# Memory-head softmax weights of a hybrid decoder trunk: transposed by DMA as two planes of 16-bit halves instead of on TensorE

## The chip, the cores and the metric

The kernel runs as one program on one core of a Trainium2 chip. The metric is the time of one execution in microseconds (us) of device time; a smaller time is better. The engines are named as in the profile: PE is TensorE (PEld its weight loads), DVE is VectorE, ACT is ScalarE, POOL is GpSimd, SP is SyncE, which issues nearly all DMAs of this kernel. Lines such as L1320 are lines of the kernel before.

## What is computed

Two decoder layers on 512 tokens of width 1024, all in fp32: a half-step SwiGLU, a mixing block of three attention branches (8 stick-breaking heads, 8 forgetting heads, 4 memory heads), another half-step SwiGLU. The change is in the memory heads. Cut to what matters of the reference:

```python
def _memory_attention(q, k, v):        # 4 heads of width 128, 512 queries, 256 memory rows
    z = jnp.einsum('bhqd,bhkd->bhqk', q, k).astype(jnp.float32) * (q.shape[-1] ** -0.5)
    p = jax.nn.softmax(z, axis=-1)
    return jnp.einsum('bhqk,bhkd->bhqd', p.astype(v.dtype), v)
...
for l in range(DEPTH):                 # DEPTH = 2
    ...
    k_mem, v_mem = jnp.split(mem_n @ w_mem_kv[l], 2, axis=-1)
    o_mem = _memory_attention(_split_heads(q_mem, N_MEM_HEADS), _split_heads(k_mem, N_MEM_HEADS),
                              _split_heads(v_mem, N_MEM_HEADS))
```

So there are 2 layers x 4 heads = 8 memory heads in the program.

## The kernel before

**Precision.** A product of two fp32 matrices is made of three matmuls of rounded parts (`mm3`, L212 to L214): high x high, high x low, low x high. Whatever enters a product is first taken apart by `split`: ACT casts the value to its high part (L182), DVE subtracts that from the value for the low part (L183). With a scale the two lines are L185 and L186.

**The mixing block.** Long products (queries, keys, values, gates) are jobs of a queue `Q`; each job loads its weights (`raw_`), takes them apart (`wh_`, `wl_`, four buffers each) and runs its matmuls. Attention heads are generators that are woven between the jobs: a head yields `("wait", us)` where it expects other engines to need that long, and the weaver then puts so many us of matmuls of the jobs into PE's program before it goes on with the head. The waits are numbers in the code, not measured at run time. Most of the order of ACT, DVE and SP comes out of the scheduler that lays out the program; at run time each engine takes its instructions strictly in that order.

**A memory head** (`mem_head`). Its 512 x 256 scores lie in two PSUM banks (`zm`), each of two blocks of 128 queries x 256 memory rows. DVE finds the maxima (L1300, L1301), ACT makes the exponentials with their sums (L1304), DVE divides (L1306, L1309): the weights `pm`, two tiles of 128 x 512. Then comes a wait W_MM0. The second product needs the weights with memory rows on partitions, so TensorE transposes them: eight 128 x 128 blocks against an identity (L1320) into two PSUM banks, which `split` takes apart into the tile `ptm`. After a wait W_MM1 six matmuls (`pvm`) multiply `ptm` with the values `mv`, and `split` writes the head's output `om`.

**The order of the heads** (`mems`). The scores of head i+1 go before the rest of head i. In the last head, at its last wait, the program turns to the first stick-breaking head: jobs are run until that head's q and k are there, ACT's function table is changed to the sigmoid's (`functions`, an ACT_TABLE_LOAD at L196), and its scores (`zs`, L1210) are started.

**The stick-breaking heads** use a DMA for their transposes already. `turn_out` (L1152) has ACT copy the 16-bit halves of the words into two planes, `turn_over` (L1161) has SP issue a DMA that transposes both planes, and ACT joins the halves into words again (L1237):

```python
    def turn_out(words, w, planes):
        both = words[:, :w].bitcast(U16).rearrange("p (k h) -> p h k", h=2)
        nc.scalar.copy(planes[:, :w].bitcast(U16).rearrange("p (h k) -> p h k", h=2), both)
    def turn_over(planes, w, over):
        nc.sync.dma_start_transpose(over[:, :w].bitcast(U16).rearrange("p (r q) -> p r q", q=P), planes[:, :w].bitcast(U16))
```

Of the kernel before, what the change touches and what calls it, by code (L numbers as in the profile page):

```python
# [12 lines left out]
U16 = mybir.dt.uint16  # L13
# [5 lines left out]
P = 128  # L19
# [4 lines left out]
def kernel(  # L24
# [38 lines left out]
    nc = tc.nc  # L63
    _, S, D = x.shape
    M = mem.shape[1]
    L = w_in.shape[0]
    NT = S // P
    ND = D // P
    MT = M // P
# [4 lines left out]
    NMH = 4  # L74
# [24 lines left out]
    def tmp(name):  # L99
        return sb.tile([P, S], F32, tag="f32t", bufs=8, name=name)  # L100
# [3 lines left out]
    def stile(shape, tag, name, dt=F32R):  # L104
        return sb.tile(shape, dt, tag=tag, bufs=BUFS[tag], name=name)
# [4 lines left out]
    def pbank(tag, name):  # L110
        return ps.tile([P, S], F32, tag=tag, bufs=4, name=name)
# [67 lines left out]
    def split(h_ap, l_ap, src, scale=None, later=False):  # L179

        if scale is None:
            both = [nc.scalar.copy(h_ap, src)]  # L182
            make = lambda: nc.vector.tensor_tensor(l_ap, src, h_ap.bitcast(F32), ALU.subtract)  # L183
        else:
            both = [nc.scalar.activation(h_ap, src, AF.Copy, scale=scale)]  # L185
            make = lambda: nc.vector.scalar_tensor_tensor(l_ap, src, scale, h_ap.bitcast(F32), ALU.mult, ALU.subtract)  # L186
        if later:
            return make
        both.append(make())
        if Q.pinned:  # L190
            for ins in both:
                tc.keep_in_program_order(ins)
        return both
# [16 lines left out]
    def mm3(pt, lh, ll, rh, rl, start, stop, free=False):  # L210

        nc.tensor.matmul(pt, lh, rh, start=start, stop=False, skip_group_check=free)  # L212
        nc.tensor.matmul(pt, lh, rl, start=False, stop=False, skip_group_check=free)  # L213
        nc.tensor.matmul(pt, ll, rh, start=False, stop=stop, skip_group_check=free)  # L214
# [934 lines left out]
# [4 lines that stand above are left out]
# [6 lines left out]
    def turn_over(planes, w, over):  # L1159

        nc.sync.dma_start_transpose(over[:, :w].bitcast(U16).rearrange("p (r q) -> p r q", q=P), planes[:, :w].bitcast(U16))  # L1161
# [125 lines left out]
    def mem_head(q, ks, vs, hd, ot, name, begun):  # L1287
        scale = P ** -0.5
        pts = []
        for i2 in range(NT // 2):  # L1290
            pz = pbank("z", f"z{name}_{i2}")
            for e in range(2):
                i = 2 * i2 + e
                qs = slice(i * P, (i + 1) * P)
                kk = ks[hd // 2]
                mm3(pz[:, e * M:(e + 1) * M], q[:, 0, qs], q[:, 1, qs],
                    kk[:, 0, hd % 2], kk[:, 1, hd % 2], e == 0, e == 1)
            st = sb.tile([P, 4], F32, tag="st4", bufs=4, name=f"st{name}_{i2}")
            p = tmp(f"p{name}_{i2}")
            nc.vector.tensor_reduce(st[:, 0:2], pz[:].rearrange("p (e m) -> p e m", e=2), AX.X, ALU.max, negate=True)  # L1300
            nc.vector.tensor_scalar(st[:, 0:2], st[:, 0:2], scale, None, ALU.mult)  # L1301
            for e in range(2):
                c = slice(e * M, (e + 1) * M)
                nc.scalar.activation(p[:, c], pz[:, c], AF.Exp, bias=st[:, e:e + 1], scale=scale,  # L1304
                                     accum_out=st[:, 2 + e:3 + e])
            nc.vector.reciprocal(st[:, 2:4], st[:, 2:4])  # L1306
            for e in range(2):
                c = slice(e * M, (e + 1) * M)
                nc.vector.tensor_scalar(p[:, c], p[:, c], st[:, 2 + e:3 + e], None, ALU.mult)  # L1309
            pts.append(p)  # L1310
        yield ("pe", 1.3)
        yield ("wait", W_MM0)
        begun()
        tri = stile([P, 2, MT * S], "tri", "pt" + name)
        for kt in range(MT):
            pt = pbank("z", f"pt{name}_{kt}")
            for i in range(NT):
                a = (i % 2) * M + kt * P
                tc.keep_in_program_order(
                    nc.tensor.transpose(pt[:, i * P:(i + 1) * P], pts[i // 2][:, a:a + P], ident[:]))  # L1320
            c = slice(kt * S, (kt + 1) * S)
            split(tri[:, 0, c], tri[:, 1, c], pt[:])
        yield ("pe", 0.9)
        yield ("wait", W_MM1)
        pv = pbank("mm", "pv" + name)
        for kt in range(MT):
            c = slice(kt * S, (kt + 1) * S)
            vc = slice((hd % 2) * P, (hd % 2 + 1) * P)
            v = vs[hd // 2]
            mm3(pv[:], v[:, 0, kt, vc], v[:, 1, kt, vc], tri[:, 0, c], tri[:, 1, c], kt == 0, kt == MT - 1)  # L1330
        split(ot[:, 0], ot[:, 1], pv[:])
        yield ("pe", 1.3)

    W_SB0, W_SB1, W_SB2 = 7.0, 7.0, 5.0
    W_FX0, W_FX1 = 6.5, 4.7
    W_MM0, W_MM1 = 6.0, 6.0
    W_K = 4.0

    FOX = (2, 3, 0, 1)
# [28 lines left out]
    def mixing(l, src, ks, vs, rest, dst):  # L1368
# [177 lines left out]
        def run():  # L1546
            Q.until(marks["first"])
            for i in range(NT):
                nc.sync.dma_start(hsave[i], hT[i][:])
            st["o", 2] = [blk("o", f"om{l}_{i}") for i in range(NMH)]  # L1550

            def mems():
                def head(i):
                    Q.until(marks["qm", i // 2])
                    return mem_head(st["qm"][i], ks, vs, i, st["o", 2][i], f"m{l}_{i}",
                                    lambda: Q.until(marks["values"]))


                def part(g):
                    for kind, us_ in g:  # L1560
                        yield (kind, us_)
                        if kind == "wait":
                            return
                gen = head(0)
                yield from part(gen)
                for i in range(NMH):
                    if i + 1 < NMH:
                        following = head(i + 1)
                        yield from ((k_, u_) for k_, u_ in part(following) if k_ == "pe")
                    for kind, us_ in gen:  # L1570
                        if kind == "wait" and i + 1 == NMH:

                            Q.past(marks[0, 0], W_K, marks[0, 1])
                            functions("sigmoid_and_others")
                            st["direct"] = True
                            begun[0, 0] = stick(0, 0)
                            yield next(begun[0, 0])
                        yield kind, us_
                    gen = following

            def stick(p, j):
                return stick_head(st["q", 0, p], st["k", 0, p], st["v", 0, p // 2], p % 2, j, st["cut"], st["o", 0][p],
                                  f"s{l}_{p}_{j}")

            def pre(at, j):

                if j == 2:
                    at, j = at + 1, 0
                p = FOX[at] if at < NP else None
                if (p, j) not in fx and ("k", 1, p) in st:  # L1590
                    fx[p, j] = fox_pre(st["q", 1, p], st["k", 1, p], j, 2 * p + j, st["cs"], f"{l}_{p}_{j}")

            def fox(at, j):
                pre(at, j)
                p = FOX[at]
                return fox_head(st["q", 1, p], st["k", 1, p], st["v", 1, p // 2], p % 2, j, fx[p, j], st["o", 1][p],
                                f"f{l}_{p}_{j}", lambda: pre(at, j + 1))

            begun, fx = {}, {}
            st["cut"] = cuts(f"{l}")  # L1600
            st["o", 0] = [blk("o", f"o{l}_0_{p}") for p in range(NP)]
            Q.weave(mems(), marks[0, 1])
            for p in range(NP):
                Q.past(marks[0, p], W_K, limits[p][0])
                for j in range(2):
                    Q.weave(begun.pop((p, j), None) or stick(p, j), limits[p][j])
            functions("natural_log_exp_and_others")
            st["direct"] = False
            st["o", 1] = [blk("o", f"o{l}_1_{p}") for p in range(NP)]
            for at, p in enumerate(FOX):  # L1610
                Q.past(marks[1, p], W_K, limits[NP + at][0])
                for j in range(2):
                    Q.weave(fox(at, j), limits[NP + at][j])
            Q.until(limits[-1][-1])
# [112 lines left out]
    for l in LAYERS:  # L1727
        i, mn = 3 * l, []
# [43 lines left out]
```

## Time and profile before

| what | us |
|---|---|
| time, median of 3 runs | 2339.55 |
| lowest and highest of them | 2337.33, 2340.01 |
| time of the profiled execution | 2342.67 |
| its span, first to last instruction | 2340.9 |
| PE busy in it (matmuls) | 2322.9 |
| DVE busy | 1764.2 |
| ACT busy | 1509.8 |
| POOL busy | 81.2 |
| memory heads of layer 0, first scores to last output product | 384.6 to 445.0 |
| memory heads of layer 1, the same | 1574.8 to 1605.9 |

The span is what the trace covers; the time of an execution has some 1.8 us around it. Busy time counts an instruction from its start to its end. On PE and on ACT the next instruction can start before the one ahead has ended, so what an instruction costs its engine is the distance from its start to the next one's start. An idle time is shown with what ended it. In the groups, the columns are line, engine, operation, tile written and tiles read, shape, count, then busy us and mean ns of one, then idle us just before and its cause.

### The profile page before, as it was taken

The numbers are of one execution on the slowest core, as the hardware profiler recorded it, in microseconds if no ns is written. First come the engines' busy times: TensorE is split into PE (matmuls) and PEld (weight loads), VectorE is DVE, ScalarE is ACT, GpSimd is POOL, SyncE is SP. The second block draws the span as 40 slices with busy tenths as digits, with TensorE's granted clock in tenths as the row PEclk, the third lists the DMA queues.
The fourth block names the chain that finished last, engine by engine and source line by source line (L and its number), as shares of the span: only waits on it lengthen the run. The fifth ranks groups of instructions, "written<-read, shape, count | busy, mean of one in ns | idle before, by whom it ended". The sixth has DMA issues, their size and how long they took to land.

```text
span 2340.9 us, 30650 instructions
## 1 busy us (share of the span) xinstructions
PE 2322.9 (99%) x11463; PEld 1960.2 (84%) x11463; DVE 1764.2 (75%) x2253; ACT 1509.8 (64%) x2216; POOL 81.2 (3%) x182
## 2 busy tenths in 40 slices
PE   9999999999999999999999999999999999999998
PEld 7888888888888888888898888888888888888887
DVE  8877877566777688878798788765677767887785
ACT  6677465577756556775656774655787674667744
POOL 0000000000111000000000000000001100000000
PEclk9999999999999999999999999999999999999999
DMA  6667454344423555674646665544444236466744
GB/s 207 190 176 221 146 189 141 93 115 114 122 73 105 187 186 164 185 199 152 226 144 186 196 185 179 185 114 95 119 105 116 81 118 200 160 195 176 220 138 144
DMA packets 340344, 365.44 MB, mean 156 GB/s; under 512 B 120778, under 2 KB 231650, under 8 KB 340196
## 3 DMA queue, kind: packets, MB, share of 16 engines
q1 hardware_dynamic: 340100, 363.46, 52.0%
q8 instruction: 90, 1.47, 0.3%
q14 instruction: 58, 0.48, 0.1%
q0 software_dynamic: 96, 0.03, 0.0%
HBM read 319.39 MB, written 16.78 MB: 144 GB/s over the span
## 4 chain that ended last, share of the span: by engine, by line
PE 85%; DMA 5%; ACT 4%; DVE 3%; issue 2%; DVEq 0%; SPq 0%; ACTq 0%
PE pg L213 4%; PE pg L212 4%; PE pg L214 4%; PE pda L213 3%; PE pda L212 3%; PE pda L214 3%; PE pdc L213 3%; PE pdc L212 3%; PE pdc L214 3%; PE pb L213 1%; PE pb L212 1%; PE pb L214 1%; PE pq L213 1%; PE pq L212 1%; PE pq L214 1%
## 5 line engine op out<-in xcount | busy, mean ns | idle before, releaser
L212 PE MATMUL pg<-us_a,wh_wg 128*128 128x512 f32 x384 | 150.4, 392 | 0.0
L213 PE MATMUL pg<-us_a,wh_wg 128*128 128x512 f32 x384 | 149.7, 390 | 0.0
L214 PE MATMUL pg<-us_a,wl_wg 128*128 128x512 f32 x384 | 149.6, 390 | 0.0
L183 DVE TENSOR_TENSOR wl_da<-raw_da,wh_da 128x1024 fp32r<-128x1024 f32 x50 | 60.8, 1223 | 44.6 <-ACT wh_da L182 44.4
L183 DVE TENSOR_TENSOR wl_dc<-raw_dc,wh_dc 128x1024 fp32r<-128x1024 f32 x50 | 61.0, 1223 | 44.1 <-ACT wh_dc L182 44.1
L213 PE MATMUL pdc<-wl_dc,ahc 128*128 128x512 f32 x224 | 87.7, 392 | 0.0
L213 PE MATMUL pda<-wl_da,aha 128*128 128x512 f32 x224 | 87.6, 391 | 0.0
L214 PE MATMUL pdc<-wh_dc,alc 128*128 128x512 f32 x224 | 87.2, 389 | 0.0
L214 PE MATMUL pda<-wh_da,ala 128*128 128x512 f32 x224 | 87.2, 389 | 0.0
L212 PE MATMUL pdc<-wh_dc,ahc 128*128 128x512 f32 x224 | 86.6, 390 | 0.5 <-ACT pdc L895 0.5
L212 PE MATMUL pda<-wh_da,aha 128*128 128x512 f32 x224 | 86.5, 389 | 0.0
L186 DVE SCALAR_TENSOR_TENSOR wl_wg<-raw_wg,wh_wg 128x1024 fp32r<-128x1024 f32 x48 | 58.7, 1223 | 35.8 <-ACT wh_wg L185 35.6
L214 PEld LDWEIGHTS pg<-us_a,wl_wg 128*128 128x128 f32 x384 | 72.1, 188 | 15.1
L212 PEld LDWEIGHTS pg<-us_a,wh_wg 128*128 128x128 f32 x384 | 72.1, 188 | 14.2
L213 PEld LDWEIGHTS pg<-us_a,wh_wg 128*128 128x128 f32 x384 | 72.1, 188 | 14.2
L182 ACT CAST wh_da<-raw_da 128x1024 fp32r<-128x1024 f32 x50 | 52.1, 1050 | 46.9 <-PE pda L214 19.4
L182 ACT CAST wh_dc<-raw_dc 128x1024 fp32r<-128x1024 f32 x50 | 52.3, 1049 | 46.0 <-DMA raw_dc<-in_ffn_w_down_dram 13.9
L182 ACT CAST wh_uc<-raw_uc 128x1024 fp32r<-128x1024 f32 x44 | 46.4, 1054 | 34.5 <-PE pwc1g L214 7.7
L182 ACT CAST wh_ua<-raw_ua 128x1024 fp32r<-128x1024 f32 x44 | 46.2, 1052 | 30.2 <-PE pwa0g L214 7.6
L183 DVE TENSOR_TENSOR wl_uc<-raw_uc,wh_uc 128x1024 fp32r<-128x1024 f32 x44 | 53.7, 1220 | 14.5 <-ACT wh_uc L182 14.5
L183 DVE TENSOR_TENSOR wl_gc<-raw_gc,wh_gc 128x1024 fp32r<-128x1024 f32 x40 | 48.5, 1221 | 20.3 <-ACT wh_gc L182 20.3
L1237 ACT COPY pws<-ts 128x1024 uint16<-128x1024 uint16 (+1 forms) x64 | 55.4, 914 | 12.2 <-DMA ts<-ns 11.9
(643 smaller groups left out, 7921.1 us busy)
## 6 DMA issues: line engine op xcount, KB each, us to landing
raw_da<-in_ffn_w_down_dram SPq DMA_DIRECT2D x66, 512.0 KB, 5.3
raw_dc<-in_ffn_w_down_dram SPq DMA_DIRECT2D x66, 512.0 KB, 4.6
raw_ga<-in_ffn_w_gate_dram SPq DMA_DIRECT2D x52, 512.0 KB, 4.7
raw_ua<-in_ffn_w_up_dram SPq DMA_DIRECT2D x52, 512.0 KB, 4.5
raw_gc<-in_ffn_w_gate_dram SPq DMA_DIRECT2D x52, 512.0 KB, 4.1
raw_uc<-in_ffn_w_up_dram SPq DMA_DIRECT2D x52, 512.0 KB, 4.4
raw_wg<-in_w_gate_dram SPq DMA_DIRECT2D x48, 512.0 KB, 3.6
raw_wo<-in_w_out_dram SPq DMA_DIRECT2D x24, 512.0 KB, 3.7
```

The source lines that it names most:

```text
L182: both = [nc.scalar.copy(h_ap, src)]
L183: make = lambda: nc.vector.tensor_tensor(l_ap, src, h_ap.bitcast(F32), ALU.subtract)
L186: make = lambda: nc.vector.scalar_tensor_tensor(l_ap, src, scale, h_ap.bitcast(F32), ALU.mult, ALU.subtract)
L212: nc.tensor.matmul(pt, lh, rh, start=start, stop=False, skip_group_check=free)
L213: nc.tensor.matmul(pt, lh, rl, start=False, stop=False, skip_group_check=free)
L214: nc.tensor.matmul(pt, ll, rh, start=False, stop=stop, skip_group_check=free)
L1237: nc.scalar.copy(block_words(word, i), over[:, :, c:c + i + 1])
```

## The change

TensorE's transposes of the memory heads go. Instead each of a head's two weight tiles is copied by ACT into planes of 16-bit halves (`turn_out`, new tile `pn`), transposed by a DMA (`turn_over`) back into `pm`, joined by ACT into words again in `pn` (the new line L1322), and then split from there. `ptm` has its columns in another order (query pair, memory tile, query), so the six matmuls of `pvm` read it through a stepped view. A third wait, W_MM2 of 4.0, stands between split and product; the wait at which the first stick-breaking head begins is now this one.

```diff
         yield ("pe", 1.3)
         yield ("wait", W_MM0)
         begun()
+        planes = []
+        for i2, p in enumerate(pts):
+            planes.append(tmp(f"pn{name}_{i2}"))
+            turn_out(p, S, planes[-1])
+            turn_over(planes[-1], S, p)
+        yield ("wait", W_MM1)
         tri = stile([P, 2, MT * S], "tri", "pt" + name)
-        for kt in range(MT):
-            pt = pbank("z", f"pt{name}_{kt}")
-            for i in range(NT):
-                a = (i % 2) * M + kt * P
-                tc.keep_in_program_order(
-                    nc.tensor.transpose(pt[:, i * P:(i + 1) * P], pts[i // 2][:, a:a + P], ident[:]))
-            c = slice(kt * S, (kt + 1) * S)
-            split(tri[:, 0, c], tri[:, 1, c], pt[:])
-        yield ("pe", 0.9)
-        yield ("wait", W_MM1)
+        for i2, (over, word) in enumerate(zip(pts, planes)):
+            nc.scalar.copy(word[:].bitcast(U16).rearrange("p (k h) -> p h k", h=2),
+                           over[:].bitcast(U16).rearrange("p (h k) -> p h k", h=2))
+            c = slice(i2 * S, (i2 + 1) * S)
+            split(tri[:, 0, c], tri[:, 1, c], word[:])
+        yield ("wait", W_MM2)
         pv = pbank("mm", "pv" + name)
         for kt in range(MT):
-            c = slice(kt * S, (kt + 1) * S)
             vc = slice((hd % 2) * P, (hd % 2 + 1) * P)
             v = vs[hd // 2]
-            mm3(pv[:], v[:, 0, kt, vc], v[:, 1, kt, vc], tri[:, 0, c], tri[:, 1, c], kt == 0, kt == MT - 1)
+            th, tl = (tri[:, part].rearrange("p (i k q) -> p k i q", k=MT, q=P)[:, kt] for part in range(2))
+            mm3(pv[:], v[:, 0, kt, vc], v[:, 1, kt, vc], th, tl, kt == 0, kt == MT - 1)
...
-    W_MM0, W_MM1 = 6.0, 6.0
+    W_MM0, W_MM1, W_MM2 = 6.0, 6.0, 4.0
...
-                        if kind == "wait" and i + 1 == NMH:
+                        if (kind, us_) == ("wait", W_MM2) and i + 1 == NMH:
                             Q.past(marks[0, 0], W_K, marks[0, 1])
                             functions("sigmoid_and_others")
```

How the instructions stand now is shown at two places of layer 0; layer 1 has the same order. In the tile names below, the last number only tells buffers apart; `pm_3_0` and `pnm_3_0` are the first weight tile of the last head (head 3) and its plane, `ptm_3` that head's split weights, `pvm_3` its product, `om_2` the output of head 2, `zs_0_0_3` the first scores of the first stick-breaking head, `q_0_1` and `k_0_1` queries and keys of the next pair of heads.

The first place is ACT between the outputs of head 2 and the first sigmoids of the stick-breaking head. Before:

```order
L182 CAST om_2_3330<-pvm_2_3742 128x512
L182 CAST ptm_3_3751<-ptm_3_0_3752 128x512
L182 CAST ptm_3_3751<-ptm_3_1_3759 128x512
L182 CAST v_0_0_0_3695<-pv_0_0_0_3696 128x4x2x64
L185 ACTIVATE wh_wg_2_0_0_3677<-raw_wg_2_0_0_3495 128x1024
L185 ACTIVATE wh_wg_2_0_4_3683<-raw_wg_2_0_4_3587 128x1024
L182 CAST v_0_0_1_3771<-pv_0_0_1_3772 128x4x2x64
L196 ACT_TABLE_LOAD
L1216 ACTIVATE ns_0_0_3_3850<-zs_0_0_3_3846 128x512
```

And now, from the last cast of head 2's weights on:

```order
L182 CAST ptm_2_3802<-pnm_2_1_3751 128x512
L185 ACTIVATE q_0_1_3818<-pq_0_1_3786 64x512
L1322 COPY pnm_3_0_3857<-pm_3_0_3724 128x2x512
L182 CAST wh_v_0_2_0_3823<-raw_v_0_2_0_3620 128x1024
L182 CAST om_2_3330<-pvm_2_3848 128x512
L182 CAST k_0_1_3875<-pk_0_1_3835 64x512
L182 CAST ptm_3_3882<-pnm_3_0_3857 128x512
L1322 COPY pnm_3_1_3860<-pm_3_1_3740 128x2x512
L1216 ACT_TABLE_LOAD
L1216 ACTIVATE ns_0_0_3_3894<-zs_0_0_3_3890 128x512
L182 CAST k_0_1_3875<-pk_0_1_3835 64x512
L182 CAST ptm_3_3882<-pnm_3_1_3860 128x512
```

The two joins of head 3 (L1322), a load of a function table that belongs to L1216, and the sigmoid itself now stand ahead of the second cast of `ptm_3`; the load of L196 follows right behind this piece, so that there are two loads where there was one. On DVE the scan of the stick-breaking head (L1222) and a low part of `k_0_1` now stand ahead of the second low part of `ptm_3`:

```order
L183 TENSOR_TENSOR ptm_3_3882<-pnm_3_0_3857,ptm_3_3882 128x512
L1222 SCALAR_TENSOR_TENSOR ns_0_0_3_3894<-ns_0_0_3_3894,cut_3332 128x511
L183 TENSOR_TENSOR k_0_1_3875<-pk_0_1_3835,k_0_1_3875 64x512
L183 TENSOR_TENSOR ptm_3_3882<-pnm_3_1_3860,ptm_3_3882 128x512
```

The second place is PE at the last head's product. Before, its last matmuls ahead of it are those of the job for `k_0_1`, and the scores `zs` lie 27 long matmuls earlier:

```order
L1210 MATMUL zs_0_0_3_3846<-k_0_0_3670,q_0_0_3578 128x512 x2
L1210 MATMUL zs_0_0_2_3856<-k_0_0_3670,q_0_0_3578 128x384 x2
L1210 MATMUL zs_0_0_1_3866<-k_0_0_3670,q_0_0_3578 128x256 x4
L212 MATMUL pq_0_1_3823<-us_a_1_2947,wh_q_0_1_3491 128x512
L213 MATMUL pq_0_1_3823<-us_a_1_2947,wh_q_0_1_3491 128x512
```

Now:

```order
L212 MATMUL pvm_2_3848<-ptm_2_3802,mv_1_3171 128x512
L213 MATMUL pk_0_1_3835<-us_a_1_2947,wh_k_0_1_3525 128x512
L214 MATMUL pk_0_1_3835<-us_a_1_2947,wl_k_0_1_3526 128x512
L213 MATMUL pvm_2_3848<-ptm_2_3802,mv_1_3171 128x512
...
L1210 MATMUL zs_0_0_3_3890<-k_0_0_3603,q_0_0_3520 128x512 x2
L1210 MATMUL zs_0_0_2_3900<-k_0_0_3603,q_0_0_3520 128x384 x2
L1210 MATMUL zs_0_0_1_3910<-k_0_0_3603,q_0_0_3520 128x256 x4
L1210 MATMUL zs_0_1_3_4117<-k_0_0_3603,q_0_0_3520 128x512 x2
L212 MATMUL pvm_3_3923<-ptm_3_3882,mv_1_3171 128x512
L212 MATMUL pg_2_0_3948<-us_a_0_2946,wh_wg_2_0_0_3610 128x512
L213 MATMUL pvm_3_3923<-ptm_3_3882,mv_1_3171 128x512
```

The jobs for q and k are used up ahead of `pvm_2`; between the products of heads 2 and 3 only the scores `zs` are left (the four rows left out are the rest of `pvm_2`). On SP eight pairs of transposing DMAs stand between the weight loads, each pair behind loads that were there before.

## The prediction

> **What bounds the kernel now.** I read the page's busy times first, then the windows around the memory heads of both layers (columns: length, busy us of PE, PEld, DVE, ACT, POOL with counts, granted clock, DMA share, GB/s).
>
> ```profile
> PE 2322.9 (99%) x11463; PEld 1960.2 (84%) x11463; DVE 1764.2 (75%) x2253; ACT 1509.8 (64%) x2216; POOL 81.2 (3%) x182
> ...
> 375.00:400.00 25.00, 25.00 (x128) 21.30 (x127) 16.43 (x34) 13.11 (x31) 0.09 (x1) 1.00 0.40 106
> 400.00:425.00 25.00, 25.00 (x156) 22.43 (x155) 16.76 (x36) 12.41 (x32) 2.46 (x5) 1.00 0.30 85
> 425.00:450.00 25.00, 25.00 (x139) 21.92 (x138) 15.40 (x20) 17.40 (x26) 1.04 (x1) 1.00 0.42 103
> 1565.00:1590.00 25.00, 25.00 (x170) 23.01 (x169) 17.14 (x36) 12.63 (x32) 2.45 (x5) 1.00 0.18 54
> ```
>
> PE is busy 25.00 of 25.00 us at a granted clock of 1.00, and the list of PE's waits has no entry there. So a matmul less is time saved one for one, and any wait of PE is lost one for one. ACT has half its time free (12.4 to 17.4 of 25), and before the change it is the one that waits for PE:
>
> ```profile
> 424.49 0.59 ACT L182 CAST om<-pvm 128x512 fp32r<-128x512 f32 x1 [2.42 <-PE pvm L214]
> 430.04 1.06 ACT L185 ACTIVATE wh_wg<-raw_wg 128x1024 fp32r<-128x1024 f32 x1 [3.49 <-PE pv L1125]
> 433.03 1.28 ACT L196 ACT_TABLE_LOAD   x1
> 436.72 0.60 ACT L1216 ACTIVATE ns<-zs 128x512 f32<-128x512 f32 x1 [2.40 <-PE zs L1210]
> ```
>
> The table load of 1.28 us lies in such a gap: ACT still waits 2.40 us for PE after it.
>
> **What goes.** The chain shows the eight transposes of a head (start, length in the chain):
>
> ```profile
> 394.44 0.87 PE ptm L1320 x8
> 404.93 0.87 PE ptm L1320 x8
> 415.41 0.87 PE ptm L1320 x8
> ```
>
> 8 heads x 0.87 = **7.0 us** off PE. (A head's two PSUM splits go too, but two splits of the same size come back, from SBUF.)
>
> **What comes on ACT.** Rows for the new operations:
>
> ```profile
> L1152 ACT COPY ns<-ts 128x1024 uint16<-128x1024 uint16 x16 | 16.8, 1048 | 0.1
> L1237 ACT COPY pws<-ts 128x1024 uint16<-128x1024 uint16 x16 | 21.6, 1352 | 5.7 <-DMA ts<-ns 5.7
> L822 ACT COPY hra<-tra0u 128x1024 uint16<-128x1024 uint16 x16 | 21.5, 1360 | 7.6 <-DMA tra0u<-tha0u 7.5
> L1161 SPq DMA_TRANSPOSE ts<-ns x48: 1209/1232/2306, 441.9 to 1776.6; - x48
> DMA to landing us min/median/max: 2.7/3.2/5.8
> 396.76 1.06 ACT L182 CAST wh_v<-raw_v 128x1024 fp32r<-128x1024 f32 x1
> 397.70 0.50 ACT L1304 ACTIVATE pm<-zm,stm 128x256 f32<-128x256 f32 x1
> ```
>
> Taking a tile apart costs 1.05 us (L1152, the same instruction). The join does not exist in this shape; both copies that write every second half-word of 1024 take 1.36, the one that writes densely 1.05. I take 1.36, since the join writes stepped; 1.05 is the lower end. A DMA lands 3.2 us after its issue (2.7 to 5.8). In a row of ACT instructions the next one starts 0.1 before the last one's end (1.06 long, next after 0.94), so I count length less 0.1: turn-out 0.95, join 1.26, cast of 1024 0.95, cast of 512 0.49. Each head adds 2 x 0.95 + 2 x 1.26 = 4.4 us to ACT, 35 us in all. Beside free time this costs nothing; the question is whether ACT is through before PE comes to `pvm`. Every `pvm` matmul now reads both query pairs, so even the first needs **both** casts, where before it needed the first only.
>
> **The last head.** The rows of PE that fix how long the matmuls take, and of ACT and DVE what stands in the new order:
>
> ```profile
> 395.85 0.39 PE L212 MATMUL pqm<-us_a,wh_qm 128*128 128x512 f32 x1
> 396.08 0.39 PE L213 MATMUL pqm<-us_a,wh_qm 128*128 128x512 f32 x1
> 417.51 0.28 PE L1123 MATMUL pv<-wh_v,us_a 128*128 128x256 f32 x1
> 418.22 0.28 PE L1123 MATMUL pv<-wh_v,us_a 128*128 128x256 f32 x1
> 436.23 1.28 PE zs L1210 x8
> 579.81 1.28 ACT L196 ACT_TABLE_LOAD   x1
> 581.10 0.58 ACT L182 CAST k<-pk 64x512 fp32r<-64x512 f32 x1
> 437.42 1.22 DVE L1222 TENSOR_TENSOR_SCAN ns<-ns,cut 128x511 f32<-128x511 f32 x1 [3.02 <-ACT ns L1216]
> L183 DVE TENSOR_TENSOR ptm<-ptm,ptm 128x512 fp32r<-128x512 f32 x16 | 10.7, 684 | 0.3 <-ACT ptm L182 0.3
> ```
>
> A matmul of 512 columns takes 0.227 us start to start, one of 256 takes 0.118 (six in 0.71). From the first matmul of `pvm_2` to that of `pvm_3` PE now has 1 + 2 + 5 long matmuls (1.8), the eight of `zs` (1.28) and two more of 512 (0.45), with 0.2 for a low part: **3.7 us**. ACT's twelve rows shown above run from the cast that frees `pvm_2` to the one that frees `pvm_3`: q 0.49, join 1.26, wh_v 0.95, om 0.49, k 0.49, cast 0.49, join 1.26, table load 1.28, sigmoid 0.5, k 0.49, and 0.49 from cast to cast: **8.2 us**. PE waits 8.2 - 3.7 = 4.5. Then the second matmul needs the low part, which DVE makes behind the scan: sigmoid 0.6, scan 1.13, k 0.6, subtraction 0.68 = 3.0 from the sigmoid's start, against 0.5 + 0.49 + 0.59 + 0.45 (two matmuls) = 2.0 on PE: 1.0 more. Last head: **5.5 us** per layer. There is a floor: even an ACT that stood idle at `om_2` would have the eight rows from there on ahead of it (5.7 us to the end of the last cast) against 1.6 us of PE's `zs`, so 4.1 + 1.0 are lost at least.
>
> The Trainium skill, page "ScalarE: Activation LUTs", section "What ACT_TABLE_LOAD costs", gives 1283 ns for the load and 1380 ns for a drain, 2.66 us together. The trace agrees with the load alone: 579.81 to the next instruction at 581.10 is 1.29 with no gap. By the page's total the last head would lose 1.4 more per layer, and the time would be 2353.4.
>
> **The other heads.** The same count, from the place after which ACT runs with no gap but the DMA. Rows for its start and for the exponentials:
>
> ```profile
> 393.76 1.41 DVE L1300 TENSOR_REDUCE stm<-zm 128x2 f32<-128x512 f32 x2 [0.76 <-PE zm L214]
> 395.09 0.29 DVE L1301 TENSOR_SCALAR stm<-stm 128x2 f32<-128x2 f32 x2
> ...
> 406.36 0.49 ACT L1304 ACTIVATE pm<-zm,stm 128x256 f32<-128x256 f32 x1
> ...
> 406.82 0.49 ACT L1304 ACTIVATE pm<-zm,stm 128x256 f32<-128x256 f32 x1
> ```
>
> An exponential takes 0.46 start to start.
> Head 0: the end of `zm_1` at 394.3 and the reduction let ACT start after 1.1 us. Four exponentials and a weight cast 2.75, turn-out to its end 1.05, DMA 3.2, join 1.36, cast 0.49, wh_q 0.95, join 1.26, q 0.49, cast to its end 0.59, hand-overs 0.3: 13.5. PE has 51 long matmuls (11.6) and eight of 256 (0.9): 12.5. Wait **1.0**.
> Head 1, from the end of `pvm_0`: om 0.49, four exponentials 1.85, turn-out 1.05, DMA 3.2, join 1.26, k 0.49, cast 0.49, join 1.26, v 0.49, cast 0.59, hand-overs 0.4, and 0.2 by which a matmul's end lies behind the next one's start: 11.8. PE has 14 x 0.227 + 66 x 0.118 = 11.0. Wait 0.8, and the low part comes 0.7 behind the cast: **1.5**.
> Head 2: ACT starts some 1.5 after `zm_3` (a subtraction stands ahead of the reduction) and needs 13.1: four exponentials, two gate casts, four turn-outs, since head 3 turns here too, v, wh_wb, q, two joins, two casts. PE has 30 x 0.118 + 46 x 0.227 = 14.0. With 0.4 for the low part and hand-overs **1.0**.
> These three hang on the DMA (0 and 1) and the join: at 2.7 and 1.05 they fall by 0.5 to 0.8 each, at the landing of a crowded stretch they grow by 2 each:
>
> ```profile
> ts<-ns SPq DMA_TRANSPOSE x3, 5.3
> ```
>
> That is the median of three transposes with weight loads issued beside them (560 to 575 us). Heads 0 and 2 have a load issued just ahead of them on SP. Weight loads behind the transposes are at most two turn-outs late; the casts that need them come many us later, hidden behind jobs already loaded. If that cover went, a load of 512 KB late by 2 us would cost as much per head.
>
> **Sum.** Per layer 1.0 + 1.5 + 1.0 + 5.5 = 9.0 of waits, 3.5 saved: +5.5. Two layers: **+11.0**. The profiled execution (2342.67, span 2340.9) would become 2353.7; it lies 3.1 above the median, and from 2339.55 I predict **2350.6**. What follows keeps its order on PE. The stick-breaking head now has 78 long matmuls and 36 of 256 (22 us) between its scores and its product; before, its weights were ready 17.4 us after the scores (436.23 to the end of the row below); so I count nothing there.
>
> ```profile
> 451.79 1.88 DVE L183 TENSOR_TENSOR pts<-pws,pts 128x640 fp32r<-128x640 f32 x2 [1.08 <-ACT pts L182]
> ```
>
> **Rivals.**
> - *ACT keeps up and only the 7.0 us show*: 2332.5, faster. For it: half of ACT is free, and the code's waits of 6 and 4 us look long. Against it: the eight rows from `om_2` on cannot start earlier, and PE has 1.6 us. Faster by over 0.2% (4.7 us, about what a measurement can tell) needs waits under 1.2 us per layer; it decides at an ACT stretch of 2.8 us where I count 5.7.
> - *Only the last head waits*: DMAs land in 2.7, the join takes 1.05. Waits 5.1 to 5.5 per layer, +3.2 to +4.0: 2342.8 to 2343.6, within 0.2%. For it: half of the DMAs land in 3.2 or less. Against it: head 2 does not hang on the DMA. The Trainium skill, page "Advanced Engine Details and Errata", section "X-Bar Transpose (TRN2)", has transposing DMAs as fast as plain ones, at 350 to 400 GB/s; worked out from that, 256 KB would move in 0.75 us (an estimate), and heads 0 and 1 would be covered. The trace has no landing under 2.7, so this gets no more of a chance.
> - *The DMAs land late, at 5.3*, behind weight loads: heads 0 to 2 lose some 5 us more per layer: 2360.6.
>
> **Chances.** Forecast (waits in all heads, 2345 to 2356) 0.60; only the last head 0.18; late DMAs 0.15; ACT keeps up 0.07. The range 2342 to 2361 takes in the first three. Faster by over 0.2% 0.07, within 0.2% 0.17, slower 0.76.
>
> **What would show it.** PE's waits should name `pvm` with ACT's `ptm`, longest 4 to 5 us, twice, and DVE's `ptm` 1 us; the window of the last head should hold PE at some 5 us less. L1322 should take 1.36. ACT's idle time before `om`, now 14.3 us, should shrink.
>
> ```profile
> L182 ACT CAST om<-pvm 128x512 fp32r<-128x512 f32 x8 | 4.7, 583 | 14.3 <-PE pvm L214 14.3
> ```
>
> I would be wrong if the scan or the sigmoid's table load started before PE's `zs`, if the first `pvm` matmul went with one cast done, or if other waits of PE turned up after the stick-breaking head begins.

## The result, and the profile after

| what | before | after |
|---|---|---|
| time, median of 5 runs (us) | 2339.55 | 2361.57 |
| lowest and highest | 2337.33, 2340.01 | 2360.00, 2363.36 |
| time of the profiled execution | 2342.67 | 2363.36 |
| ratio after / before, 95% interval | | 1.0096 (1.0082 to 1.0111) |

The change costs 22.0 us, nearly 1%, where 11.0 were forecast; 2361.57 lies just above the range. The page of after, busy times, and the list of PE's waits (who waited for whom: us in total, times, longest):

```profile
PE 2327.2 (99%) x11399; PEld 1958.3 (83%) x11399; DVE 1767.0 (75%) x2253; ACT 1547.7 (66%) x2250; POOL 83.8 (4%) x182
...
PE pvm L212 <- ACT ptm L182: 12.2, 6, 4.3
PE pvm L212 <- DVE ns L1222: 4.9, 1, 4.9
PE pvm L213 <- DVE ptm L183: 1.5, 4, 0.6
```

PE has 64 instructions fewer than before (11399 for 11463) and yet is busy 4.3 us longer, on top of 18.6 us of waits at `pvm` (the three rows of the list), none of which were there before. (The second row is put down to the scan that ended last; in layer 0 the same wait names ACT's `ptm`.) The total of the waits is close to the 18.0 of the forecast. What was not forecast is that PE gets slower. Its rows show why when the trace is cut into stretches of 3.41 us (columns as in the windows before: length, busy us of PE, PEld, DVE, ACT, POOL, granted clock, DMA share, GB/s), heads 2 and 3 of layer 0:

```profile
438.23:441.64 3.41, 1.20 (x6) 0.66 (x4) 0.24 (x1) 2.38 (x4) 0.10 (x1) 1.00 0.74 139
441.64:445.06 3.42, 3.12 (x7) 2.49 (x8) 2.00 (x4) 3.09 (x4) 0.00 (x0) 0.50 0.41 130
445.06:448.47 3.41, 2.19 (x12) 1.58 (x10) 2.85 (x4) 2.94 (x5) 1.28 (x3) 1.00 0.32 78
448.47:451.88 3.41, 0.34 (x2) 0.30 (x2) 1.52 (x2) 3.33 (x5) 0.44 (x1) 1.00 0.25 76
451.88:455.30 3.42, 2.86 (x7) 1.82 (x6) 2.96 (x5) 3.41 (x7) 1.60 (x2) 0.50 0.00 0
455.30:458.71 3.41, 3.41 (x9) 2.64 (x8) 2.69 (x6) 2.60 (x4) 0.00 (x0) 0.50 0.49 94
458.71:462.12 3.41, 3.41 (x16) 2.81 (x15) 0.00 (x0) 2.12 (x2) 0.00 (x0) 1.00 0.74 101
```

The clock is 1.00 or 0.50 and changes at the edges of these stretches only. A stretch in which PE waited most of the time (1.20 and 0.34 busy of 3.41) is followed by one at half clock; after one that was nearly all busy (3.12 of 3.42, 3.41) it is full again. A stretch that is itself at half clock can be followed by another at half after less waiting: 0.56 (2.86 busy of 3.42) was enough at 451.88. In layer 1 it is the same: 1581.70 to 1585.11, and 1622.66 to 1629.48, with 3.41 and 5.55 busy; 1581.70 lies 334 times 3.4133 after 441.64, so the stretches run on through the whole execution. What PE loses is taken as half of its busy time at half clock: (3.12 + 2.86 + 3.41 + 3.41 + 5.55) / 2 = **9.2 us**. The sum is then -7.0 + 18.6 + 9.2 = +20.8; the profiled executions differ by 20.7.

ACT at the last head of layer 0 (start, length):

```profile
446.48 0.62 ACT L182 CAST ptm<-pnm 128x512 fp32r<-128x512 f32 x1
447.00 1.33 ACT L1322 COPY pnm<-pm 128x1024 uint16<-128x1024 uint16 x1
448.35 1.28 ACT L1216 ACT_TABLE_LOAD   x1
449.64 0.60 ACT L1216 ACTIVATE ns<-zs 128x512 f32<-128x512 f32 x1
450.26 0.58 ACT L182 CAST k<-pk 64x512 fp32r<-64x512 f32 x1
450.87 0.62 ACT L182 CAST ptm<-pnm 128x512 fp32r<-128x512 f32 x1
```

The first product of head 3 starts at 451.54, behind the last of these rows. Groups and DMA issues that the prediction named (line, shape, count, busy us, mean ns, idle before; for the DMA the median us to landing):

```profile
L1322 ACT COPY pnm<-pm 128x1024 uint16<-128x1024 uint16 x16 | 21.4, 1348 | 8.3 <-DMA pm<-pnm 8.3
L182 ACT CAST om<-pvm 128x512 fp32r<-128x512 f32 x8 | 4.8, 599 | 9.8 <-PE pvm L214 9.7
pm<-pnm SPq DMA_TRANSPOSE x16, 4.3
```

The join takes 1.35 where the prediction took 1.36; ACT's idle time before `om` shrank from 14.3 to 9.8. A transpose landed 4.3 us after its issue in the median, 1.1 later than the 3.2 I took. ACT waited for that in head 2 too, which I had counted as free of the DMA. These are its two joins in layer 0, where SP issues the four transposes of heads 2 and 3 in a row:

```profile
437.19 1.35 ACT L1322 COPY pnm<-pm 128x1024 uint16<-128x1024 uint16 x1 [0.96 <-DMA pm<-pnm]
439.57 1.33 ACT L1322 COPY pnm<-pm 128x1024 uint16<-128x1024 uint16 x1 [1.03 <-DMA pm<-pnm]
```

The Trainium skill, page "TensorE: Matmul & The Clock Gate", section "Part 1: The HAM clock gate (the "warmup" mystery)", states a window of 3413 ns that runs freely, and a clock that is either full or half: the rows above agree on both. It puts the fall behind an idle window of some 3.4 us; here 1.20 us of work in a stretch of 3.41 did not prevent it.

### The profile page after: what moved, and what is told of

It is laid out like the page before. It is cut to its first block, busy times and chain, and to the rows that moved or that the text cites. A ratio compares the mean times of both kernels' runs of the same rounds, so it can differ in the third digit from the quotient of the medians.

```text
span 2361.5 us, 30585 instructions
## 1 busy us (share of the span) xinstructions
PE 2327.2 (99%) x11399; PEld 1958.3 (83%) x11399; DVE 1767.0 (75%) x2253; ACT 1547.7 (66%) x2250; POOL 83.8 (4%) x182
## 4 chain that ended last, share of the span: by engine, by line
PE 82%; DMA 6%; ACT 6%; DVE 4%; issue 2%; POOL 0%; DVEq 0%; ACTq 0%; SPq 0%
PE pg L213 4%; PE pg L214 4%; PE pg L212 4%; PE pda L213 3%; PE pda L212 3%; PE pda L214 3%; PE pdc L213 3%; PE pdc L212 3%; PE pdc L214 2%; PE pb L213 1%; PE pb L214 1%; PE pb L212 1%; DMA pm<-pnm 1%; PE pwc1g L212 1%; PE pwc1g L213 1%
## 5 line engine op out<-in xcount | busy, mean ns | idle before, releaser
L183 DVE TENSOR_TENSOR wl_ga<-raw_ga,wh_ga 128x1024 fp32r<-128x1024 f32 x40 | 48.5, 1220 | 20.6 <-ACT wh_ga L182 20.6
```

## The experiments

The theory: ACT's longer chain makes PE wait for both casts of `ptm`, and a wait that fills about half of one of the 3.41-us stretches is paid again at half clock. The rivals: the slow matmuls come from the stepped view of `ptm` or from the DMAs; or one single step (landing, join, table load) sets the waits. Each time is a median beside runs of the kernel before on the same chip. All kernels but `waits_only` are made from the changed one; "after" is the changed kernel itself. With each edit the scheduler lays out the order of ACT, DVE and SP anew, so a run can change more than its edit.

**1. Waits and nothing else, in the kernel before (`waits_only`).** It has no DMA transposes, no joins and no stepped view.

```diff
+        late = sb.tile([P, 3 * P], F32, tag="late", bufs=1, name="late" + name) if hd < 3 else None
+        for _ in range({'0': (7, 14, 17), '1': (8, 15, 20)}[name[1]][hd] if hd < 3 else 0):
+            nc.gpsimd.tensor_copy(late[:], tri[:, 1, S:S + 3 * P].bitcast(F32))
...
         pv = pbank("mm", "pv" + name)
+        if hd < 3:
+            tc.keep_in_program_order(nc.tensor.transpose(pv[:, :P], late[:, :P], ident[:]))
```

> The kernel before, with waits and nothing else: TensorE keeps its transposes, no DMA, no joins, no stepped view. GpSimd, which is idle there, copies the low part of ptm into a spare tile 7, 14 and 17 times (layer 0, heads 0 to 2) and 8, 15 and 20 times (layer 1), and one extra transpose of that tile, overwritten by pvm, makes PE wait for it ahead of the product. Output the same. Theory (any wait of PE is paid twice where it fills about half of one of the 3.41-us stretches in which the clock is granted): waits of some 1.4 to 5 us, 15 us in all; behind those above 2.1 us the clock is 0.50 for 3.4 or 6.8 us, its edges a multiple of 3.41 us apart over the whole run; the time is before + the waits + 1.7 for each stretch at half, so 2338.4 + 15 + 5 to 12 = 2358 to 2366. Rival (the half clock comes from the transposing DMAs or the view): the clock stays at 1.00 and the time is 2338.4 + the waits = 2353.

Measured 2371.87 against 2337.97, +33.9. Two of the waits in layer 0 of its timeline, and the stretches around them:

```profile
404.00 0.33 PE L1330 MATMUL pvm<-ident,latem 128*128 128x128 f32 x1 [2.06 <-POOL latem L1325]
419.33 0.33 PE L1330 MATMUL pvm<-ident,latem 128*128 128x128 f32 x1 [2.09 <-POOL ts L1215]
...
400.92:404.34 3.42, 1.36 (x10) 1.12 (x9) 1.55 (x5) 1.02 (x4) 2.71 (x6) 1.00 0.64 186
404.34:407.75 3.41, 3.41 (x12) 2.87 (x12) 0.83 (x3) 0.59 (x1) 0.00 (x0) 0.50 0.00 0
...
414.58:417.99 3.41, 2.66 (x18) 2.23 (x17) 2.18 (x4) 0.55 (x1) 3.04 (x7) 1.00 0.53 154
417.99:421.41 3.42, 2.08 (x12) 1.78 (x13) 1.01 (x5) 1.35 (x5) 1.20 (x4) 1.00 0.02 5
421.41:424.82 3.41, 3.41 (x25) 3.15 (x24) 2.81 (x6) 3.41 (x9) 0.00 (x0) 1.00 0.00 0
```

A wait of 2.06 us that lay in one stretch halved the next; one of 2.09 that an edge cut in two cost nothing beyond itself. In layer 1 the pair was 2.27 and 2.17, with the same outcome. GpSimd's copies took 0.57 us each, so the waits were longer than meant, 27.4 us in all (the longest 8.9 and 9.8); half of PE's busy time at half clock is 7.2; 34.6 in all, and 33.9 were measured. The halved clock comes from waiting, whatever PE waits for: here it waits for GpSimd, with no stepped view and no transposing DMA in the memory heads. The expected total was too low because the copies were mis-sized; the rival's 1.00 throughout is excluded.

**2. Dummy matmuls in the waits (`fill`).**

```diff
         pv = pbank("mm", "pv" + name)
+        vw = vs[hd // 2][:, 0].rearrange("p t c -> p (t c)")
+        for _ in range((6, 4, 10, 18)[hd]):
+            tc.keep_in_program_order(nc.tensor.matmul(pv[:], vw[:, 0:P], vw, start=True, stop=True, skip_group_check=True))
```

> The changed kernel with dummy matmuls of 512 columns (6, 4, 10 and 18 for heads 0 to 3) written into the bank of pvm ahead of its first product, which overwrites them; the output stays the same. They keep PE busy in the waits and nothing else moves on ACT, DVE or the DMAs. Theory (the waits let the granted clock fall to half, and that costs 10.4 us beside the waits): pvm starts when it started, the clock stays at 1.00 in every window of the memory heads, the pvm matmuls fall from 0.54 back to 0.39 us, and the time is 2361.6 - 10.4 = 2351 (2349 to 2354, since a dummy too many costs 0.23). Rival 1 (the stepped view of ptm, or the transposing DMAs beside it, make the matmuls slow): the clock rows or the matmuls stay as they are and the time is 2360 to 2364. Rival 2 (PE's waits are longer than the list says): 2356 to 2362 at full clock.

Measured 2360.37 against 2338.44, +21.9. The theory's 2349 to 2354 was missed; the number lies in the range of rival 1. The waits were not where I had put the dummies: in heads 1 and 2 of layer 0 the transposes landed later after their issue than in after, so that ACT's joins waited longer for them (0.84 and 0.96 there):

```profile
417.44 1.37 ACT L1322 COPY pnm<-pm 128x1024 uint16<-128x1024 uint16 x1 [2.32 <-DMA pm<-pnm]
...
441.38 2.52 ACT L1322 COPY pnm<-pm 128x1024 uint16<-128x1024 uint16 x2 [2.84 <-DMA pm<-pnm]
```

So 8.7 us of waits were left beside 76 dummies (17.3 us), and 6.5 us were lost at half clock behind the waits of three heads. Why those transposes landed later wasn't followed, so the time of this run doesn't tell the theories apart. What its profile does show: at the last head, where the dummies left no wait, no fall of the clock followed in either layer, though view and DMAs were there; rival 1 had the clock rows stay as they were.

**3. Other work for the last wait (`supply`).**

```diff
-                merge(2, w_br_mem, i)
+                merge(2, w_br_mem, i, apart=i == 0)
...
-            Q.weave(mems(), marks[0, 1])
+            Q.weave(mems(), marks["gates", 2])
```

> The changed kernel with other work for the last wait: the sigmoid gates of the first memory merge become a job of their own (48 matmuls of 512 columns, 10.9 us) that may run before the last head's product. Theory: the wait of 4.3 to 4.9 us and the low part's 0.3 to 0.6 go in both layers (10.0 us), and the half clock behind them (14 us at half, 7 us) with it: 2361.6 - 17 = 2344.5 (2341 to 2348); the waits of heads 0 to 2 and two short falls of the clock stay. Rival (waits alone count, the rest is the stepped view): 2351.5. If ACT is the bound of the whole stretch, the wait turns up later instead, at the product of the gates with om: 2355 or more.

Measured 2352.39 against 2338.44, +13.95; 8.1 less than after's +22.0, instead of 17. The number lies next to the rival's 2351.5, but not by the rival's mechanism: the last head's waits went in both layers, and with them all stretches at half clock in the memory heads but one (443.89 to 447.31). 8.5 us of waits stayed in heads 0 to 2. But the gates were missing later, at the stick-breaking heads (before: 1.4 and 0.6 in these two rows):

```profile
PE pvs L1171 <- DVE pts L183: 5.2, 8, 0.9
...
PE pvs L1171 <- ACT pts L182: 1.2, 1, 1.2
```

Those 4.4 us, and a stretch at half clock behind three of those waits (594.09 to 597.50), are a wait that only moved. That explains about 6 of the 9 us that are missing; the rest stays open.

**4. The table load earlier (`early_table`).** The two lines that change ACT's table for the stick-breaking head are moved from the last head's last wait to the one before it.

```diff
+                        if (kind, us_) == ("wait", W_MM1) and i + 1 == NMH:
+                            functions("sigmoid_and_others")
+                            st["direct"] = True
...
-                            functions("sigmoid_and_others")
-                            st["direct"] = True
```

> The changed kernel with ACT's table change written ahead of the last head's joins, so that there is one load again and it stands before the output of head 2; the sigmoid then follows both casts of ptm. Theory: one load (1.28) and the scan ahead of the second low part leave the last head; its wait falls from 4.9 and 5.2 to about 4.0 a layer, still long enough for the clock to fall: 2361.6 - 2 = 2359.5 (2357 to 2361). Rival (the second table load is what makes the last head late): the wait falls to 2.5 or less and the clock falls hardly: 2350 to 2355.

Measured 2355.28 against 2338.44, +16.8. The last head still waits 3.1 and 4.3 us (after: 4.9 and 5.2 with the low part), and 7.0 us are lost at half clock. The last head's waits fell by 2.7 us in all, more than the 2 of the theory; the rival's 2.5 us or less did not come. The time lies 1.7 below the theory's range and just above the rival's. The run doesn't price the load by itself, since ACT's order changed with it. In layer 0 both joins of head 3 now stand behind `om_2`, which starts at 446.06:

```profile
447.02 2.54 ACT L1322 COPY pnm<-pm 128x1024 uint16<-128x1024 uint16 x2
```

In after the first of them stood ahead of it (442.53 and 445.52). So a load and a sigmoid (1.28 and 0.60) left ACT's stretch from `om_2` to the last cast and a join came in: 5.3 us instead of 6.0.

**5. The last head on TensorE again, heads 0 to 2 by DMA (`three_heads`).** For head 3 the code of before stands (both versions are in the listings above).

```diff
+        if hd < NMH - 1:
...
+        else:
+            tri = stile([P, 2, MT * S], "tri", "pt" + name)
+            for kt in range(MT):
...
```

> The changed kernel with the last head's transposes back on TensorE, as before the change, and heads 0 to 2 by DMA. Theory: the last head's wait (4.3 + 0.6 and 4.9 + 0.3) and the half clock behind it go; 6 x 0.87 = 5.2 is still saved; heads 0 to 2 keep some 8.5 us of waits and one to three stretches at half, 1.7 each: 2338.4 - 5.2 + 8.5 + 1.7 to 5.1 = 2343.4 to 2346.8. Rival (heads 0 to 2 are harmless and the last head alone costs): 2334 to 2336.

Measured 2345.50 against 2337.97, ratio 1.0030 (1.0019 to 1.0042). PE's waits:

```profile
PE pvm L212 <- ACT ptm L182: 8.2, 6, 2.3
...
PE pvm L213 <- DVE ptm L183: 0.6, 2, 0.3
```

8.8 us of waits and one stretch at half (1.7), less 5.2, make +5.3; +7.5 were measured. The time is within the range stated. Heads 0 to 2 lose more than they save even by themselves: the rival falls.

**6. Joins, turn-outs, or both on DVE.** The joins alone (`join_dve`):

```diff
-            nc.scalar.copy(word[:].bitcast(U16).rearrange("p (k h) -> p h k", h=2),
-                           over[:].bitcast(U16).rearrange("p (h k) -> p h k", h=2))
+            nc.vector.tensor_copy(word[:].bitcast(U16).rearrange("p (k h) -> p h k", h=2),
+                                  over[:].bitcast(U16).rearrange("p (h k) -> p h k", h=2))
```

> The changed kernel with the joins of L1322 on DVE instead of ACT. Theory (ACT's chain makes PE wait): ACT loses 2 x 1.26 a head, the last head's wait at pvm goes, but DVE's queue gets two joins ahead of the low part of k, and the scores of the next pair wait for POOL's copy of k instead, 3 to 4 us; waits 7 to 8 us a layer against 9.3, with one fall of the clock a layer behind the longest: 2355 (2350 to 2359). Rival (the landing of the DMA alone sets the waits of heads 0 to 2, the table load that of head 3): heads 0 to 2 as they were, 2359 to 2362.

The turn-outs alone (`turn_dve`):

```diff
+    def turn_out_dve(words, w, planes):
+        both = words[:, :w].bitcast(U16).rearrange("p (k h) -> p h k", h=2)
+        nc.vector.tensor_copy(planes[:, :w].bitcast(U16).rearrange("p (h k) -> p h k", h=2), both)
...
-            turn_out(p, S, planes[-1])
+            turn_out_dve(p, S, planes[-1])
```

> The changed kernel with the turn-outs alone on DVE, joins on ACT: the counterpart to the joins alone on DVE (+12 us against before) and to both (-3). Theory (one chain; what is taken off ACT ahead of the DMA brings the landing forward by up to 2 x 0.95 a head and lets head 3's joins go before the output of head 2): waits of 2 to 4 us a layer, none above 1.7, one stretch at half clock at the most: 2338 - 7 + 4 to 8 + 0 to 1.7 = 2335 to 2341. Rival (the join's 1.35 us, twice, ahead of the last casts, is what makes the last head late): its wait of 4 us stays, 2350 or more.

Both edits (`dve_both`):

> The changed kernel with turn-outs and joins on DVE (0.76 us each there, by the run with the joins on DVE) and none on ACT. Theory (the chain on ACT is what PE waits for): the waits fall to 0.2 to 1 us a head, 2 to 3 us a layer with the last head, too short for the clock to fall; 7.0 saved: 2338.4 - 7 + 4 to 6 = 2336.4 (2334 to 2340), faster than or as fast as before. Rival (the landing of the DMA, 3 us and more, sets the waits whatever engine copies): 4 us a layer in heads 0 to 2 remain and a stretch or two at half: 2341 to 2345.

Both, but the first tile of each head turned out by ACT (`(turn_out_dve if i2 else turn_out)`, `dve_most`):

> As the last one, but the first tile of each head is turned out by ACT and the second by DVE, side by side; joins on DVE. Theory: chains some 0.4 us shorter than with both on DVE, 0.5 to 1 us less of waits a layer: 2335.4 (2333 to 2339). Rival (the landing of the DMA): 2341 to 2345.

| kernel | time | before | ratio, 95% interval | waits at `pvm` | at half clock |
|---|---|---|---|---|---|
| joins on DVE (`join_dve`) | 2350.49 | 2338.44 | 1.0046 (1.0032 to 1.0059) | 13.5 | 3.1 |
| turn-outs on DVE (`turn_dve`) | 2343.49 | 2337.43 | 1.0025 (1.0015 to 1.0034) | 7.1 | 0 |
| both (`dve_both`) | 2335.20 | 2337.97 | 0.9990 (0.9982 to 0.9999) | 4.3 | 0 |
| both, but one turn-out (`dve_most`) | 2338.63 | 2337.97 | 1.0003 (0.9994 to 1.0011) | 5.9 | 0 |

The last column is half of PE's busy time at half clock in the memory heads. The same two copies on DVE, in the kernel with both there (line, count, ns min/median/max, first and last start):

```profile
L1161 DVE COPY pnm<-pm x16: 672/680/693, 395.8 to 1588.0; 128x1024 uint16<-128x1024 uint16 x16
L1326 DVE COPY pnm<-pm x16: 736/755/1411, 400.8 to 1596.1; 128x1024 uint16<-128x1024 uint16 x16
```

These are 0.68 and 0.76 against ACT's 1.05 and 1.35. PE's waits with both there:

```profile
PE pvm L212 <- ACT ptm L182: 2.7, 4, 1.6
...
PE pvm L213 <- DVE ptm L183: 1.6, 3, 1.1
```

The kernel is faster than before by 2.8 us, with an interval that ends just below 1: -7.0 + 4.3 gives -2.7, which is closer than such a sum can be relied on (see the sums below). So the landing of the DMA, which did not change (4.2 us in the median), is no floor. With joins alone on DVE the waits I expected at the next scores did not come; they stayed at `pvm`, and the last head, whose wait was to go, still waits 2.95 us in each layer. That the time came out within the stated range was luck.

The turn-outs alone did better than the joins, as only their theory had it. With the joins still on ACT, the last head has no wait at `pvm` in either layer, because ACT is through with the last cast of `ptm_3` before it comes to `om_2` (layer 0):

```profile
442.59 0.62 ACT L182 CAST ptm<-pnm 128x512 fp32r<-128x512 f32 x1
...
444.19 0.59 ACT L182 CAST om<-pvm 128x512 fp32r<-128x512 f32 x1
```

So it is the joins' place behind `om_2` that made the last head late, and not their length alone. The time missed the range by 2.5. Head 2 of layer 0 waited 2.40 us where none above 1.7 was forecast; an edge cut that wait, and no fall of the clock followed. A new wait of 1.25 us in each layer, for the low part of `om` at the first memory merge, was not foreseen, and 3 to 4 us of the +6.1 are not explained by PE's waits in that profile. One turn-out left on ACT was worse, not better, than none, against its theory; its time is within the stated range.

**7. Both on DVE, with other waits in the code (`dve_w1`, then `dve_w2`).**

```diff
-    W_MM0, W_MM1, W_MM2 = 6.0, 6.0, 4.0
+    W_MM0, W_MM1, W_MM2 = 6.0, 7.0, 4.0
```

> Both on DVE, and the second wait of a head (between the DMA's issue and the joins) at 7.0 us instead of 6.0, so that PE has four more matmuls of the jobs ahead of each product. Theory: waits of 4.0 us in both layers fall to 1 to 3; 2332.5 to 2335, 1 to 2.5 below both on DVE. Rival (the jobs used earlier are missing at the last head): its wait grows by what the others lose, 2335 to 2338.

Measured **2334.24** against 2337.43, ratio 0.9988 (0.9979 to 0.9997), the fastest kernel of the study. Its waits at `pvm`:

```profile
PE pvm L213 <- DVE ptm L183: 1.2, 3, 0.5
...
PE pvm L212 <- ACT ptm L182: 0.5, 1, 0.5
```

1.7 us are left, none long enough to halve the clock. Here the stepped view can be read at full clock (`pvm`, ns min/median/max), first in before and then in this kernel:

```profile
L214 PE MATMUL pvm<-ptm,mv x16: 389/389/393, 402.4 to 1605.6; 128*128 128x512 f32 x16
```

```profile
L214 PE MATMUL pvm<-ptm,mv x16: 389/393/398, 405.8 to 1599.6; 128*128 128x512 f32 x16
```

4 ns for 48 matmuls are 0.2 us: the stepped view costs nothing that counts. With waits of 6.5, 6.5 and 3.0 us instead:

> Both on DVE, waits of 6.5, 6.5 and 3.0 us instead of 6.0, 6.0 and 4.0: the same sum, shifted to where the DMA flies. Theory: 2333 to 2335.5. Rival (the low parts of ptm come too late with 3.0 between cast and product): 2335 to 2338.

Measured 2336.48 against 2337.43, ratio 0.9995 (0.9986 to 1.0003): the rival's range. One wait of 1.74 us for a low part, in one stretch, was enough for a stretch at half.

**The sums.** Each from its own profile, less the 7.0 (5.2 in `three_heads`, none in `waits_only`) saved, beside the difference of the medians:

| kernel | waits at `pvm` | half clock | other terms | sum | measured |
|---|---|---|---|---|---|
| after | 18.6 | 9.2 | | +20.8 | +22.0 |
| waits_only | 27.4 | 7.2 | | +34.6 | +33.9 |
| fill | 8.7 | 6.5 | 17.3 dummies | +25.5 | +21.9 |
| supply | 8.5 | 3.4 | 4.4 at `pvs`; 1.7 of the half clock is there too | +9.3 | +13.95 |
| early_table | 16.7 | 7.0 | | +16.7 | +16.8 |
| join_dve | 13.5 | 3.1 | | +9.6 | +12.05 |
| three_heads | 8.8 | 1.7 | | +5.3 | +7.5 |
| turn_dve | 7.1 | 0 | 2.5 at the merge | +2.6 | +6.1 |
| dve_both | 4.3 | 0 | | -2.7 | -2.8 |
| dve_most | 5.9 | 0 | | -1.1 | +0.7 |
| dve_w1 | 1.7 | 0 | | -5.3 | -3.2 |
| dve_w2 | 3.4 | 1.7 | | -1.9 | -0.95 |

PE's waits elsewhere add up to 10.3 us in the profile of before and to between 4.6 and 11.2 in the others; a sum from one execution can be no closer than a few us. Before's profiled execution lies 3.1 above its median, and its waits elsewhere are among the largest; profile against profile, `dve_both` differs from before by -7.0 and `dve_w1` by -10.7. The sums carry the order of the kernels and the large terms, not single microseconds.

## Why the prediction was right in part: the waits, but not their price

- **8 x 0.87 = 7.0 off PE**: right. With the waits nearly gone (`dve_w1`), 3.2 of it show, and 5.3 by that kernel's sum.
- **ACT, the order, and where PE waits**: right. The longest waits are at `pvm` of the last heads, behind join, table load, sigmoid and cast, as counted.
- **9.0 of waits per layer**: 18.6 measured for 18.0, but this is two errors that nearly cancel, and so partly luck. The last head was put too high (11.0 for both layers, 10.0 measured), heads 0 to 2 too low (7.0, measured 8.5). Over both layers head 0 has 3.5 for 2.0, head 1 has 1.2 for 3.0 and head 2 has 3.8 for 2.0. "Head 2 does not hang on the DMA" was wrong: ACT waited there 2.0 us for landings in layer 0 and 0.85 in layer 1. Transposes landed in 4.3 us where I took 3.2; how much of the excess that explains in each head wasn't shown. The rival with late landings gave 2360.6, next to the measured time, but by luck: it needs 28 us of waits and no fall of the clock.
- **"Any wait of PE is lost one for one"**: this is the step that failed. The rows I quoted show a granted clock of 1.00 in every window, and I took it for a constant; but they are windows in which PE hardly waits. Half clock behind the longer waits took 9.2 us more, a term that the sum did not have; with it and the measured waits the sum is 20.8 instead of 11.0. `waits_only` shows the fall with waits alone, and `dve_both` and `dve_w1` show none in the memory heads with view and DMAs but short waits. No rival had this mechanism, so the range ended at 2361.
- **The direction**: right, with its reason. The floor of 4.1 + 1.0 at the last head stood on the order in which ACT has eight rows from `om_2` on. They took 6.0 us in layer 0 (445.52 to 451.49), where I put 5.7, whose own terms add up to 5.6; the last head waited 4.9 and 5.2. `dve_both` has waits of 0.4 there and `turn_dve` none: the floor belonged to that order.
- **The table load as two loads**: right, 1.28 each and nothing more, and in `early_table`, with one of them gone, the last head still waits 3.1 and 4.3 us.

## What to carry to other kernels

Where the bounding engine is TensorE, count a wait by its place as well as by its length: several short ones cost their length, one of 2 us can cost 3.7, and which it is depends on where the stretches fall. When work leaves the busy engine for one with "half its time free", what counts is how much stands in that engine's queue ahead of the result at the one place where it is due; share it out, get it ahead of what waits for the busy engine, or put more work ahead of the consumer, and see that this work isn't missing further on.

## What the runs showed of the hardware

- The granted clock is 1.00 or 0.50, for whole stretches of 3.41 us that run on through the execution (in `waits_only` two falls are 1174.18 us apart, 344 times 3.4133).
- A stretch of 3.41 us at full clock in which PE waited 2.0 us or more was followed by half clock in every such case between 20 and 2320 us of these profiles (17 of 17); up to 1.5 us it never was. Between them both occurred: 1.56, 1.72 and 1.74 were followed by a fall, 1.75, 1.78 and 1.80 were not. So a wait of 2.95 us (`join_dve`, layer 1) cut by an edge cost nothing beyond itself, and one of 1.74 (`dve_w2`) cost 1.7 more.
- A copy of 1024 half-words that splits or joins planes takes DVE 0.68 or 0.76 us and ACT 1.05 or 1.35: here the engine with more busy time was the better place.
